# Attention, RWKV-7 and MoE block on one core: side steps without products ordered apart from PSUM places, x for the norm loaded piece by piece

## The chip, the core and the metric

One core of one Trainium2 chip runs the whole program. The metric is the device time of one execution in microseconds (us); lower is better. A change of 0.5% is 5.3 us here.

The core has engines that run beside each other, each with a queue of its own: PE (matrix products, with its weight loads listed as PEld), DVE, ACT and POOL (elementwise work, each with its own strengths), SP (issues DMAs). An engine takes its instructions strictly in the order of its queue; one that waits for data, for a place in SRAM or in PSUM (the accumulators of PE) holds up whatever stands behind it. ACT, POOL and SP issue DMAs too ("ACTq", "POOLq", "SPq" in the rows).

## The reference

One layer on `x` of 256 tokens by 2048 channels, all in float32:

```python
h = rms_norm(x, g_mix)
proj = h @ w_in                                   # all columns of both head groups
y_dsa = dsa_mixer(q, k, v, q_idx, k_idx, w_idx)   # indexer, top-k keys, rope, softmax
y_rwkv = rwkv7_mixer(r, d_w, k, v, d_a, d_g, ...) # state scan over the tokens, 16 heads x 64
x = x + concat([y_dsa, y_rwkv]) @ w_out
x = x + hier_moe(rms_norm(x, g_ffn))              # top-1 of 4 groups, top-2 of 4 experts in it
```

`rms_norm(x)` is x times `rstd`, one number per token: one over the root of the mean square over the 2048 channels. The kernel multiplies x by the weights first and by `rstd` behind the product, so the product need not wait for `rstd`.

## The kernel before

**Two stages.** Up to about 585 us the kernel does the projection, both mixers and the output projection; after that the MoE, expert pair by expert pair. The change touches the first stage alone.

**The stream.** The first stage is one long list of tasks, `stream`. A task of the first kind multiplies x (already scaled by the gain, in `hT0` to `hT3`) with one block of 128 columns, 12 products of 128x256 per task and four tasks per block; a task of the second kind takes 512 columns, 6 products of 128x512 per task and 16 tasks per 512 columns. Each product is made of three, since each operand is split into a high and a low part. `drive` walks over the tasks. It loads the raw weights with SP, 512 KB at a time (two tasks), into three places in turn (`RA` has two, `RB` one; line 210); it splits each half into a high part (ACT, the cast of line 222) and a low part (DVE, the subtraction of line 223), which stand in four halves of `W20` and `W21`, so that the split runs at most four tasks ahead of PE; and it lets PE multiply (`pp`, line 146).

**Side chains.** All else in that stage is done by Python generators ("chains") whose steps are laid between the tasks: `spread` (the norm's `rstd`), the low-rank parts, indexer and attention, and per RWKV block b an early part, a solve and a late part. The class `Order` holds a modelled time `t` that each product moves on. A step ends with `yield`: a number is a delay, so many microseconds of `t` until the next step, a name is an event to wait for. `run_ready` goes through the chains in the list's order and lets the first one run whose time has come; `ready` also asks for a place in PSUM: there are three for side products (`BANKS`), taken in turn, and one is counted free some time after the step that used it. The order on PE is exactly the order in which this plan writes the products; SP's loads and the steps on ACT, DVE and POOL follow the program too, but a scheduler may move them past each other.

**The norm.** `spread` (lines 288 to 312) loads x in four pieces of 512 KB by POOL (line 296) into `yr` and `qT`, which nothing else uses yet; ACT squares each piece into `vt` and sums along it (line 300); DVE and ACT make `rstd` (lines 302 to 304); DVE lays it on a diagonal (line 307); PE spreads it over the partitions (`rps`); ACT copies that to `rsB`. From then on each block's result waits for `rsB` and not for anything of `spread` again. On POOL, the loads of x share the queue with the rotary tables (lines 354 to 358).

**Solves.** `solve(b)` (lines 679 to 696) is a triangular solve on POOL, some 62 small operations; the result goes to DRAM (`dout`, line 695). `solved(b)` waits `SOLVE_US` of modelled time, and then has SP load it back into `XT` (line 702), four loads that stand in SP's queue between the weights'; `rwkv_late(b)` waits for that.

**Prefetch for the MoE.** After the last early part, `leave_rwkv` (lines 1159 to 1180) loads the first chunks of the experts' weights, 1 MB each; from then on `prefetch_step` (lines 1184 to 1193) is called at each weight load and adds a chunk when `PACE` says so. Each of these loads is gated: POOL copies one element of the current half of W (`pace["w"]`, set in `split`) into the new place before the load is issued, so that the load is not issued before ACT's cast into that half is done, and ACT's next cast into that half waits in turn for the copy (line 1145).

```python
c[0], c[1] = self.t + y, None              # a delay
c[0], c[1] = self.t, y                     # the name of an event
return None if r is None else max(r, self.free[self.place] or 0.0)
```

Of the kernel before, what the change touches and what calls it, by code (L numbers as in the profile page):

```python
# [9 lines left out]
F32 = mybir.dt.float32  # L10
F32R = mybir.dt.float32r
AF = mybir.ActivationFunctionType
# [5 lines left out]
P = 128  # L18
# [4 lines left out]
SB = 2  # L23
# [10 lines left out]
WARM = 14  # L34
BANKS, EMPTIED = 3, 2.0
PACE0 = 8.0
PACE, SOLVE_US, RSTD_US = 2.2, 39.0, 16.1
Y = [8.0, 5.6, 9.8, 1.6, 4.0, 2.6, 4.8, 5.8, 3.1, 6.0, 5.2, 3.0, 3.0, 3.1, 19.0, 5.7, 12.6, 4.4, 7.2, 4.8, 2.2, 6.6, 2.8, 6.2, 7.2, 2.2, 3.5, 0.0, 1.5, 1.1, 2.2, 16.1, 5.0, 2.2, 10.7, 10.4, 1.0, 5.0]

# [3 lines left out]
class Order:  # L45
# [18 lines left out]
    def event(self, name, delay=0.0):  # L64
        self.ev[name] = self.t + delay

    def add(self, gen):
        self.chains.append([0.0, None, gen])

    def ready(self, c):  # L70

        r = self.inputs(c)
        return None if r is None else max(r, self.free[self.place] or 0.0)

    def inputs(self, c):
        if c[1] is not None:
# [56 lines left out]
def block_kernel(ctx: ExitStack, tc: tile.TileContext, a: dict, dbg=None):  # L133
    nc = tc.nc
    PE, ACT, DVE, POOL, SP = nc.tensor, nc.scalar, nc.vector, nc.gpsimd, nc.sync
    SQ = POOL
    od = Order()
# [75 lines left out]
    pace = {}  # L213
# [19 lines left out]
    G = [gp.tile([P, 2048], F32, name=f"G{i}", tag=f"g{i}") for i in range(3)]  # L233
# [12 lines left out]
    state = rw.enter_context(tc.tile_pool(name="state", bufs=1, side="right"))  # L246
# [40 lines left out]

    def spread():

        yield 4.0  # L290
        part = const.tile([P, 2, 2], F32, name="part")
        xv = a["x"].rearrange("(j p) (c m) -> p j c m", p=P, c=2)
        xs = [t.rearrange("p b t -> p (b t)").rearrange("p (c m) -> p c m", c=2) for t in (yr, qT)]
        for j in range(2):
            for c in range(2):
                POOL.dma_start(out=xs[j][:, c, :], in_=xv[:, j, c, :])
                yield 1.0
        for j in range(2):
            for c in range(2):
                ACT.activation(out=vt[:, j, :], in_=xs[j][:, c, :], func=AF.Square, accum_out=part[:, j, c:c + 1])  # L300
                yield 1.0 * c
        DVE.tensor_tensor(out=rstd, in0=part[:, :, 0], in1=part[:, :, 1], op=ALU.add)
        ACT.activation(out=rstd, in_=rstd, func=AF.Ln, scale=1.0 / D, bias=eps6)
        ACT.activation(out=rstd, in_=rstd, func=AF.Exp, scale=-0.5)
        dg = temp("kd")
        for j in range(2):
            DVE.tensor_scalar(dg[:, j * P:(j + 1) * P], ident, rstd[:, j:j + 1], None, ALU.mult)
        yield 4.0
        ps = pbank("rps")
        mm(ps[:, 0:T], ones, dg)  # L310
        ACT.copy(out=rsB, in_=ps[:, 0:T])
        od.event("rsB", Y[22])

# [49 lines left out]
    yr = apool.tile([P, NB, T], F32, name="yr")  # L363
# [98 lines left out]
    def done0(ps):  # L462
# [7 lines left out]
        ACT.copy(out=SG[32:64, 2, :], in_=sgt[96:128, :])  # L470
        od.event("xb", Y[23])

    def done1(ps):
# [7 lines left out]
        for i in range(2):  # L481
            h = slice(64 * i, 64 * i + 64)
            ACT.copy(out=X1[h, i, :], in_=lo1[h, :])
            DVE.tensor_tensor(out=X1[64 - 64 * i:128 - 64 * i, i, :], in0=lo1[h, :], in1=X1[h, i, :].bitcast(F32), op=ALU.subtract)
        od.event("lo1", Y[24])

# [42 lines left out]
    def add_rwkv(b, which="krv"):  # L529
        for n, nm in enumerate("krv"):  # L530
            if nm not in which:
                continue
            def done(ps, n=n, nm=nm):
# [6 lines left out]
                shift(ps, 3 + 3 * b + n, t)  # L540
                od.event(f"{nm}{b}", Y[25])
            add_cm(3 + 3 * b + n, chain(done) if b == 0 else lambda ps, done=done: list(done(ps)))
# [12 lines left out]
    def rwkv_early(b):  # L555
# [4 lines left out]
        lh, ll = low_rank(b, 0, two_early)  # L560
        yield Y[0]
        pz = pbank("pz")
# [42 lines left out]
        r = s["r"]  # L605
# [13 lines left out]
        ACT.copy(out=rho, in_=KR[:, 1, :])  # L619

        AB = state.tile([P, 2, 4, 64], F32, name="AB", bufs=SB)
        MM = state.tile([P, 2, 4, 2, 64], F32, name="MM", bufs=SB + 1)
        pas = [pbank("pa") for _ in range(2)]
        od.emptied = 4.5
        for j in range(2):
# [12 lines left out]
        for ci in range(4):  # L638
            i = ci % 2
            ACT.dma_start(out=dr[b][0].rearrange("ci u s t -> ci s u t")[ci],  # L640
                           in_=AB[32 * ci:32 * ci + 32].rearrange("p h (j s) t -> p (h j) s t", s=2)[:, :, 0, 32 * i:32 * i + 32])
# [30 lines left out]
        for hj in range(4):  # L672
            h, j = hj // 2, hj % 2
# [7 lines left out]
    def solve(b):  # L681

        at = [tmp.tile([P, n, 32], F32, name=f"at{n}", bufs=1) for n in (8, 24)]
        xt = tmp.tile([P, 4, 32], F32, name="xt", bufs=1)
        tt = tmp.tile([P, 128], F32, name="tt", bufs=1)
        for t, r0, r1 in ((at[0], 0, 8), (at[1], 8, 32)):
            SQ.dma_start(out=t, in_=dr[b][0][:, :, r0:r1, :].rearrange("(o ci) u s t -> o (ci u) (s t)", o=1).broadcast_to([8, 16, 32 * (r1 - r0)]))
        POOL.tensor_copy(xt, xt0)
        for s_ in range(31):
            n, m = s_ // 8 + 1, 31 - s_  # L690
            tv = tt[:, 0:n * m].rearrange("p (u t) -> p u t", u=n)
            POOL.tensor_tensor(out=tv, in0=xt[:, 0:n, s_:s_ + 1].broadcast_to([P, n, m]),  # L692
                               in1=at[s_ >= 8][:, s_ % 8 if s_ < 8 else s_ - 8, s_ + 1:32].rearrange("p (o t) -> p o t", o=1).broadcast_to([P, n, m]), op=ALU.mult)
            POOL.tensor_tensor(out=xt[:, 0:n, s_ + 1:32], in0=xt[:, 0:n, s_ + 1:32], in1=tv, op=ALU.subtract)  # L694
        SQ.dma_start(out=dr[b][1].rearrange("ci w (i q) t -> q (ci w) i t", q=8), in_=xt.rearrange("p i t -> p (i t)"))
        od.add(solved(b))

    def solved(b):

        yield SOLVE_US  # L700
        for ci in range(4):
            tc.keep_in_program_order(SP.dma_start(out=XTs[b % SB][32 * ci:32 * ci + 32, :, 32 * ci:32 * ci + 32], in_=dr[b][1][ci].rearrange("u s t -> s u t")))
        od.event(f"solved{b}", Y[37])
# [107 lines left out]
    qT = apool.tile([P, 8, T], F32, name="qT")  # L811
    vt = apool.tile([P, 2, 1024], F32, name="vt")
# [179 lines left out]
    def put_heads():  # L992
        for h in range(4):
            yield f"att{h}"
            yield f"slot{YSLOTS.index(f'h{h}') // 4}"
            put_y(f"h{h}", qT[:, h, :])


    def chain(gen):
        return lambda ps: od.add(gen(ps))  # L1000
# [43 lines left out]
    od.add(kidx())  # L1044
    od.add(indexer())
    od.add(attention())
    od.add(put_heads())
    if dbg == "dsa":
        drive()
        od.finish()  # L1050
# [108 lines left out]
    def leave_rwkv():  # L1159

        yield f"early{NB - 1}"
        for i in range(2):
            load_chunk(i, True)
            yield PACE0

        x01 = mo_["x01"] = gp.tile([P, 2, 2, 512], F32, name="x01", tag="g2")
        POOL.tensor_copy(x01[0:1, 0, 0, 0:1], pace["w"][0:1, 0:1].bitcast(F32))
        for cc in range(2):
            POOL.dma_start(out=x01[:, cc], in_=a["x"].rearrange("(j p) m -> p j m", p=P)[:, :, cc * 512:(cc + 1) * 512])
        yield PACE0  # L1170
        yield f"late{NB - 1}"
        yield Y[19]
        rw.close()
        ewp[1] = ctx.enter_context(tc.tile_pool(name="ew", bufs=1, side="right", reuse_waits="tile"))
        for i in range(FIRST):
            load_chunk(2 + i)
        od.event("rw closed")
# [82 lines left out]

    c0, c1 = stream[-64:-48], stream[-48:-32]
    stream[-64:-32] = c0[:12] + c1[:8] + c0[12:] + c1[8:]
    od.add(leave_rwkv())
    drive(prefetch_step)
    od.finish()
    gF = mo_["gF"]
# [371 lines left out]
```

## Time and profile before

| what | value |
|---|---|
| median of 3 runs | 1054.12 us (1052.23 to 1056.83) |
| the profiled execution | 1053.52 us, its span 1051.7 us |
| PE busy | 1012.2 us, 96% of the span, 6476 products |
| DVE busy | 528.9 us (50%) |
| ACT busy | 387.7 us (37%) |
| POOL busy | 257.8 us (25%) |
| DMA | 298.75 MB, mean 284 GB/s |

The span runs from the first to the last instruction on the core; the execution's own time lies 1.8 us above it. PE is busy nearly all the time, so a few places where PE waits are all that a change of order can win or lose. A wait on an engine other than PE costs only where PE in the end waits for it.

### The profile page before, as it was taken

The numbers are of one execution on the slowest core, as the hardware profiler recorded it, in microseconds if no ns is written. First come the engines' busy times: TensorE is split into PE (matmuls) and PEld (weight loads), VectorE is DVE, ScalarE is ACT, GpSimd is POOL, SyncE is SP. The second block draws the span as 40 slices with busy tenths as digits, with TensorE's granted clock in tenths as the row PEclk, the third lists the DMA queues.
The fourth block names the chain that finished last, engine by engine and source line by source line (L and its number), as shares of the span: only waits on it lengthen the run. The fifth ranks groups of instructions, "written<-read, shape, count | busy, mean of one in ns | idle before, by whom it ended". The sixth has DMA issues, their size and how long they took to land.

```text
span 1051.7 us, 17181 instructions
## 1 busy us (share of the span) xinstructions
PE 1012.2 (96%) x6476; PEld 683.2 (65%) x6476; DVE 528.9 (50%) x1155; ACT 387.7 (37%) x836; POOL 257.8 (25%) x645
## 2 busy tenths in 40 slices
PE   5899999999999999999999899999999999999995
PEld 5898888889889877788877544444444444444432
DVE  5696787698978765756554313131312222221303
ACT  5666656566566754566454101010101010000001
POOL 3206676572664737002222110000000000000000
PEclk9999999999999999999999999999999999999999
DMA  8556744535454464648899798999999999999995
GB/s 286 211 180 174 203 150 136 167 114 147 134 155 139 137 189 133 235 123 289 285 324 378 314 365 352 422 419 420 420 421 419 421 420 420 419 421 420 420 405 176
DMA packets 69210, 298.75 MB, mean 284 GB/s; under 512 B 17184, under 2 KB 20048, under 8 KB 45056
## 3 DMA queue, kind: packets, MB, share of 16 engines
q1 hardware_dynamic: 54864, 248.59, 63.6%
q0 software_dynamic: 8928, 47.41, 12.7%
q10 hardware_dynamic: 5328, 1.58, 0.6%
q8 instruction: 53, 0.87, 0.3%
q14 instruction: 37, 0.30, 0.1%
HBM read 294.37 MB, written 3.15 MB: 283 GB/s over the span
## 4 chain that ended last, share of the span: by engine, by line
PE 78%; DVE 8%; DMA 5%; ACT 3%; issue 2%; POOL 2%; SPq 0%; ACTq 0%; DVEq 0%; POOLq 0%
PE pp L146 27%; PE pd L146 11%; PE gate L146 11%; PE up L146 10%; PE misc L146 6%; PE sc L146 3%; DVE W L223 3%; PE pz L146 2%; DMA RB<-wo 2%; PE py L146 2%; DMA RB<-wr 1%; POOL xt L694 1%; ACT W L222 1%; POOL tt L692 1%; DMA xT<-xT 1%
## 5 line engine op out<-in xcount | busy, mean ns | idle before, releaser
L146 PE MATMUL pp<-W,hT 128*128 128x512 f32 x768 | 190.1, 397 | 0.0
L146 PE MATMUL pp<-hT,W 128*128 128x256 f32 x1296 | 170.9, 289 | 11.8 <-DVE W L223 8.4
L223 DVE TENSOR_TENSOR W<-RA,W 128x512 fp32r<-128x512 f32 x200 | 138.3, 701 | 81.6 <-ACT W L222 80.9
L146 PEld LDWEIGHTS pp<-hT,W 128*128 128x128 f32 x1296 | 161.8, 194 | 16.2 <-DVE W L223 9.2
L222 ACT CAST W<-RA 128x512 fp32r<-128x512 f32 x200 | 121.8, 618 | 100.9 <-PE pp L146 52.2
L146 PEld LDWEIGHTS pp<-W,hT 128*128 128x128 f32 x768 | 139.8, 188 | 29.0 <-issue 0.7
L692 POOL TENSOR_TENSOR tt<-xt,at 128x24 f32<-128x24 f32 (+23 forms) x248 | 87.5, 353 | 52.5 <-DMA at<-din 33.7
L694 POOL TENSOR_TENSOR xt<-xt,tt 128x24 f32<-128x24 f32 (+23 forms) x248 | 94.4, 381 | 19.5
L146 PE MATMUL pp<-W,yT 128*128 128x512 f32 x384 | 91.3, 394 | 2.1 <-DVE W L223 2.1
L223 DVE TENSOR_TENSOR W<-RB,W 128x512 fp32r<-128x512 f32 x100 | 69.1, 696 | 48.3 <-ACT W L222 48.1
L146 PE MATMUL pd<-ew,R 128*64 128x512 f32 (+1 forms) x368 | 81.3, 580 | 2.0 <-DVE Y L1482 1.4
L222 ACT CAST W<-RB 128x512 fp32r<-128x512 f32 x100 | 61.2, 618 | 59.1 <-PE pp L146 28.3
L146 PEld LDWEIGHTS pp<-W,yT 128*128 128x128 f32 x384 | 71.0, 188 | 18.4 <-DVE W L223 3.6
L146 PE MATMUL up<-ew,R 128*64 128x512 f32 x352 | 79.3, 592 | 0.0
L146 PEld LDWEIGHTS misc<-sel,uu 128*128 128x128 f32 x512 | 60.1, 191 | 18.8 <-issue 13.8
L1491 ACT ACTIVATE Y<-pd,sv 128x512 fp32r<-128x512 f32 x31 | 21.3, 688 | 134.0 <-PE pd L146 134.0
L146 PE MATMUL misc<-sel,uu 128*128 128x128 f32 x512 | 64.9, 280 | 2.8 <-DVE R L1396 2.1
L1501 DVE TENSOR_TENSOR x<-x,sc 128x512 f32<-128x512 f32 (+1 forms) x58 | 36.2, 666 | 57.3 <-PE sc L146 57.3
L1396 DVE TENSOR_TENSOR R<-misc,gF 128x512 f32<-128x512 f32 x28 | 19.4, 692 | 87.1 <-PE misc L146 87.1
L146 PE MATMUL gate<-ew,R 128*64 128x512 f32 x272 | 61.7, 595 | 0.0
L1492 DVE SCALAR_TENSOR_TENSOR Y<-pd,sv,Y 128x512 fp32r<-128x512 f32 x31 | 23.3, 751 | 73.2 <-ACT Y L1491 73.2
L1420 ACT CAST selT<-misc 128x256 fp32r<-128x256 f32 x8 | 3.0, 372 | 153.7 <-PE misc L146 153.7
(389 smaller groups left out, 1216.4 us busy)
## 6 DMA issues: line engine op xcount, KB each, us to landing
ew<-we SPq DMA_DIRECT2D x66, 1024.0 KB, 19.9
ew<-wdn SPq DMA_DIRECT2D x38, 1024.0 KB, 19.3
ew<-we POOLq DMA_DIRECT2D x25, 1024.0 KB, 7.5
ewh<-we SPq DMA_DIRECT2D x24, 1024.0 KB, 18.2
RA<-wd SPq DMA_DIRECT2D x43, 512.0 KB, 3.8
RA<-wr SPq DMA_DIRECT2D x35, 512.0 KB, 3.9
RB<-wd SPq DMA_DIRECT2D x21, 512.0 KB, 3.7
RA<-wo SPq DMA_DIRECT2D x21, 512.0 KB, 4.6
```

The lines of the kernel that those rows point to most:

```text
L146: PE.matmul(out, lhsT=lhsT, rhs=rhs, start=start, stop=stop, skip_group_check=skip)
L222: ACT.copy(out=hi, in_=raw)
L223: DVE.tensor_tensor(out=lo, in0=raw, in1=hi.bitcast(F32), op=ALU.subtract)
L692: POOL.tensor_tensor(out=tv, in0=xt[:, 0:n, s_:s_ + 1].broadcast_to([P, n, m]), in1=at[s_ >= 8][:, s_ % 8 if s_ < 8 else s_ - 8, s_ + 1:32 ...
L694: POOL.tensor_tensor(out=xt[:, 0:n, s_ + 1:32], in0=xt[:, 0:n, s_ + 1:32], in1=tv, op=ALU.subtract)
L1396: DVE.tensor_tensor(out=t[:, a:b], in0=ps.rearrange("p (a t) -> p a t", t=P)[:, a:b], in1=gF[:, 4 * kq + a:4 * kq + b].rearrange("p (a o) ...
L1420: ACT.copy(out=selT, in_=ps[:, 0:T])
L1491: ACT.activation(out=yh, in_=pd, func=AF.Copy, scale=sv[:, 1:2])
L1492: DVE.scalar_tensor_tensor(out=yl, in0=pd, scalar=sv[:, 1:2], in1=yh.bitcast(F32), op0=ALU.mult, op1=ALU.subtract)
L1501: DVE.tensor_tensor(out=x1[j][:, ns], in0=(uu[:, j, ns] if first else x1[j][:, ns]), in1=ps, op=ALU.add)
```

## The change

- `add` takes a flag `dry`. A dry chain is one without products: `solved`, `put_heads` and `leave_rwkv`. It no longer asks for a place in PSUM before it runs, and stands at the front of the list of chains, not at its end.
- `spread` takes its x in four pieces into other places: three tiles `xs` that share their ring with `MM` (a tile of the early part), and the right half of `G1`. Each load is gated by POOL's copy of one element of the current half of W, as the prefetches are. The steps that issue the loads are 2 us of modelled time apart, and the squares are written in place of the pieces.
- Numbers: `PACE` from 2.2 to 1.8, `SOLVE_US` from 39 to 41, and five of the delays `Y`: `Y[3]` (1.6 to 2.4), `Y[8]` (3.1 to 3.4), `Y[12]` (3.0 to 3.6), `Y[16]` (12.6 to 13.2), `Y[37]` (5.0 to 4.5).

```diff
-PACE, SOLVE_US, RSTD_US = 2.2, 39.0, 16.1
-Y = [8.0, 5.6, 9.8, 1.6, 4.0, 2.6, 4.8, 5.8, 3.1, 6.0, 5.2, 3.0, 3.0, 3.1, 19.0, 5.7, 12.6, 4.4, 7.2, 4.8, 2.2, 6.6, 2.8, 6.2, 7.2, 2.2, 3.5, 0.0, 1.5, 1.1, 2.2, 16.1, 5.0, 2.2, 10.7, 10.4, 1.0, 5.0]
+PACE, SOLVE_US, RSTD_US = 1.8, 41.0, 16.1
+Y = [8.0, 5.6, 9.8, 2.4, 4.0, 2.6, 4.8, 5.8, 3.4, 6.0, 5.2, 3.0, 3.6, 3.1, 19.0, 5.7, 13.2, 4.4, 7.2, 4.8, 2.2, 6.6, 2.8, 6.2, 7.2, 2.2, 3.5, 0.0, 1.5, 1.1, 2.2, 16.1, 5.0, 2.2, 10.7, 10.4, 1.0, 4.5]
...
-    def add(self, gen):
-        self.chains.append([0.0, None, gen])
+    def add(self, gen, dry=False):
+
+        c = [0.0, None, gen, dry]
+        self.chains.insert(0, c) if dry else self.chains.append(c)
 
     def ready(self, c):
 
         r = self.inputs(c)
-        return None if r is None else max(r, self.free[self.place] or 0.0)
+        return r if r is None or c[3] else max(r, self.free[self.place] or 0.0)
...
     def spread():
 
-        yield 4.0
         part = const.tile([P, 2, 2], F32, name="part")
         xv = a["x"].rearrange("(j p) (c m) -> p j c m", p=P, c=2)
-        xs = [t.rearrange("p b t -> p (b t)").rearrange("p (c m) -> p c m", c=2) for t in (yr, qT)]
-        for j in range(2):
-            for c in range(2):
-                POOL.dma_start(out=xs[j][:, c, :], in_=xv[:, j, c, :])
-                yield 1.0
-        for j in range(2):
-            for c in range(2):
-                ACT.activation(out=vt[:, j, :], in_=xs[j][:, c, :], func=AF.Square, accum_out=part[:, j, c:c + 1])
-                yield 1.0 * c
+        xs = [state.tile([P, 1024], F32, name="xs", tag="MM", bufs=SB + 1) for _ in range(3)] + [G[1][:, 1024:2048]]
+        yield 3.0
+        for n in range(4):
+            POOL.tensor_copy(xs[n][0:1, 0:1], pace["w"][0:1, 0:1].bitcast(F32))
+            POOL.dma_start(out=xs[n], in_=xv[:, n // 2, n % 2, :])
+            yield 2.0
+        yield 1.0
+        for n in range(4):
+            ACT.activation(out=xs[n], in_=xs[n], func=AF.Square, accum_out=part[:, n // 2, n % 2:n % 2 + 1])
+            yield 1.0 * (n % 2)
...
-        MM = state.tile([P, 2, 4, 2, 64], F32, name="MM", bufs=SB + 1)
+        MM = state.tile([P, 2, 4, 2, 64], F32, name="MM", tag="MM", bufs=SB + 1)
...
-        od.add(solved(b))
+        od.add(solved(b), dry=True)
...
-    od.add(put_heads())
+    od.add(put_heads(), dry=True)
...
-    od.add(leave_rwkv())
+    od.add(leave_rwkv(), dry=True)
```

**POOL, at the start of the program** (the rows after its first memsets and loads; `cs` and `gq` are tables for the rotation, `cg` and `sg` what is made of them, `xt` the start of a solve). Lines 297 and 298 of the changed kernel are the gate's copy and the load of x. Before:

```order
L575 MEMSET G1_89 128x4
L296 DMA yr_190<-x 128x1024 x2
L296 DMA qT_214<-x 128x1024 x2
L346 DMA cs64_184<-cs64 128x128
L354 ISA
L354 TENSOR_TENSOR cg_182<-cs128_641,gq_642 128x64
```

Of the changed kernel, from the second of its last table operations on:

```order
L358 TENSOR_SCALAR sg__183<-sg__183 128x64
L690 COPY xt_986<-con_174 128x128
L298 DMA xs_222<-x 128x1024
L297 COPY xs_223<-W21_84 1x1
L358 TENSOR_SCALAR sg__183<-sg__183 128x64
L359 TENSOR_SCALAR sn64_185<-cs64_184 128x2x32
L360 COPY sn64_185<-cs64_184 128x2x32
L297 COPY xs_224<-W20_83 1x1
L297 COPY G1_89<-W20_83 1x1
L358 TENSOR_SCALAR sg__183<-sg__183 128x64
L298 DMA xs_223<-x 128x1024
L298 DMA xs_224<-x 128x1024
```

The four loads of x stood ahead of all table operations; now the first stands behind 19 of them and the last at their end, the copy of the first gate being the eighth of the operations.

**PE, around the product that spreads `rstd`** (`rps`; each row x12 is one task). Before:

```order
L146 MATMUL pp_348<-hT1_69,W20_83 128x256 x12
L146 MATMUL pp_348<-hT2_70,W21_84 128x256 x12
L146 MATMUL pp_348<-hT3_71,W21_84 128x256 x12
L146 MATMUL rps_410<-G0_88 128x256
L146 MATMUL pp_415<-hT0_68,W20_83 128x256 x12
```

Of the changed kernel:

```order
L148 MATMUL pp_351<-hT3_71,W21_84 128x256 x12
L148 MATMUL pp_419<-hT0_68,W20_83 128x256 x12
L148 MATMUL pp_419<-hT1_69,W20_83 128x256 x12
L148 MATMUL pp_419<-hT2_70,W21_84 128x256 x6
L148 MATMUL rps_455<-G0_88 128x256
L148 MATMUL pp_419<-hT2_70,W21_84 128x256 x6
```

Two and a half tasks have moved from behind `rps` to ahead of it: 14½ stand ahead of it instead of 12.

**SP, around the loads of the fourth solve's result** (`dout3`; `wr` and `wd` are weights of the stream, `lora` the low-rank weights). Before:

```order
L210 DMA RB_82<-wr 128x1024
L210 DMA RA_81<-wr 128x1024 x2
L210 DMA RB_82<-wr 128x1024
L210 DMA RA_81<-wd 128x1024
L702 DMA XT1_187<-dout3_204 32x4x32 x4
L210 DMA RA_81<-wd 128x1024
```

Of the changed kernel:

```order
L508 DMA G1_89<-lora 128x256
L212 DMA RA_81<-wr 128x1024 x2
L704 DMA XT1_187<-dout3_204 32x4x32 x4
L212 DMA RB_82<-wr 128x1024
L212 DMA RA_81<-wr 128x1024 x2
L212 DMA RB_82<-wr 128x1024
L212 DMA RA_81<-wd 128x1024 x2
```

The four loads of `dout3` go ahead of five weight loads that they stood behind.

## Rows read from the trace of the kernel before

**Rows 1.** The page's head: the span, and each engine's busy time.

```profile
span 1051.7 us, 17181 instructions
PE 1012.2 (96%) x6476; PEld 683.2 (65%) x6476; DVE 528.9 (50%) x1155; ACT 387.7 (37%) x836; POOL 257.8 (25%) x645
```

**Rows 2.** Waits by what ended them: us in total, times, longest us.

```profile
PE pp L146 <- DVE W L223: 10.5, 6, 7.0
...
PE rps L146 <- DVE G L307: 2.8, 1, 2.8
PE tps L156 <- DVE re L742: 2.2, 1, 2.2
...
PE pz L146 <- DVE R L728: 1.1, 1, 1.1
```

**Rows 3.** Timeline, the way to `rps`: start, us, engine, operation, [idle before <- what ended it].

```profile
19.78 1.06 POOL L296 DMA_DIRECT2D yr<-x  x2 [16.01 <-DMA G<-lora]
20.14 8.89 PE L146 MATMUL pp<-hT,W 128*128 128x256 f32 x72 [0.21 <-DVE W L223]
...
22.52 0.53 POOL L354 TENSOR_TENSOR cg<-cs,gq 128x64 f32<-128x64 f32 x1
...
24.48 0.76 POOL L355 TENSOR_TENSOR sg__183<-cs,gq 128x64 f32<-128x64 f32 x1
...
27.99 0.31 POOL L355 TENSOR_TENSOR sg__183<-cs,gq 128x64 f32<-128x64 f32 x1
...
29.10 1.40 DVE L223 TENSOR_TENSOR W<-RB,W 128x512 fp32r<-128x512 f32 x2 [4.03 <-ACT W L222]
...
29.93 1.45 POOL L356 TENSOR_SCALAR sg__183<-sg__183 128x64 f32<-128x64 f32 x3
...
31.71 1.06 ACT L300 ACTIVATE vt<-qT 128x1024 f32<-128x1024 f32 x1
...
35.82 0.67 PE L146 MATMUL rps<-G 128*128 128x256 f32 x2 [2.82 <-DVE G L307]
```

**Rows 4.** DMA issues: KB each, median us from issue to landing.

```profile
RB<-wr SPq DMA_DIRECT2D x18, 512.0 KB, 4.1
...
yr<-x POOLq DMA_DIRECT2D x2, 512.0 KB, 5.2
qT<-x POOLq DMA_DIRECT2D x2, 512.0 KB, 9.1
```

**Rows 5.** Timeline, the first gated chunk, behind the last solve.

```profile
415.23 0.19 POOL L1145 COPY ew<-W 1x1 f32<-1x1 f32 x1
415.45 0.62 ACT L222 CAST W<-RB 128x512 fp32r<-128x512 f32 x1 [6.41 <-POOL ew L1145]
```

**Rows 6.** Timeline, the end of the output projection on PE.

```profile
577.93 1.65 PE L146 MATMUL pp<-W,yT 128*128 128x512 f32 x6 [1.57 <-DVE W L223]
```

**Rows 7.** The chain of waits at that place: start, us, what.

```profile
567.12 9.30 DMA RB<-wo
```

**Rows 8.** Timeline around the end of the fourth solve.

```profile
232.72 0.33 SPq L210 DMA_DIRECT2D RB<-wr  x1
...
237.54 0.29 POOL L688 COPY xt<-con 128x128 f32<-128x128 f32 x1 [3.45 <-DMA dout<-xt]
...
241.59 0.62 ACT L222 CAST W<-RB 128x512 fp32r<-128x512 f32 x1 [0.81 <-PE pp L146]
```

**Rows 9.** Windows: us; busy us (count) of PE, PEld, DVE, ACT, POOL; PEclk, DMA share, GB/s.

```profile
12.40:16.40 4.00, 4.00 (x19) 3.87 (x19) 3.68 (x9) 3.63 (x9) 0.00 (x0) 1.00 1.02 393
20.50:24.50 4.00, 4.00 (x36) 4.00 (x35) 3.65 (x10) 2.40 (x5) 3.90 (x8) 1.00 0.81 271
...
775.00:800.00 25.00, 24.65 (x138) 11.63 (x135) 4.06 (x11) 1.65 (x3) 0.00 (x0) 1.00 1.01 420
1048.00:1051.70 3.70, 0.00 (x0) 0.00 (x0) 0.00 (x0) 0.00 (x0) 0.00 (x0) 0.50 0.06 13
```

**Rows 10.** Timeline, the last products of the program.

```profile
1043.58 0.74 PE L146 MATMUL sc<-Y,selT 128*128 128x256 f32 x4 [1.00 <-DVE Y L1482]
```

## The prediction, made before the changed kernel ran

> **What bounds the kernel now.** I read the page's head first: PE is busy for 1012.2 us of 1051.7 [rows 1]. A change of order can therefore only win or lose at the few places where PE waits, and the list of waits names them. The largest is `pp` behind DVE's split, 10.5 us in six waits of which 7.0 is one [rows 2], at the program's start, where the first weights have not landed; the change does not reach it. The others that it touches are 2.8 us at `rps`, 2.2 at `tps`, 1.1 at `pz` and 1.57 at the end of the output projection [rows 2, 6]. The MoE stage is dense: 24.65 of 25 us with DMA at 420 GB/s [rows 9]; none of its instructions is moved, so it shifts with the first stage. All sums are against the profiled execution, 1053.52 us, which lies 0.6 below the median of the runs, 1054.12.
>
> **Term 1, the way to `rstd`: +3.7 us.** Before, the loads of x were the first thing that POOL did at 19.78, two of them in 1.06 us, so 0.53 each, and the first table operation followed at 22.52 [rows 3]. Twelve tasks stood ahead of `rps`, eight of them behind 20.14. Six took 8.89 us, so 1.48 each [rows 3]; eight need 11.8, and `rps` could have begun at 32.0. It began at 35.82: the stretch lost 3.8 us.
> Now the tables go first. Only the load of `cs64` is ahead of them, so they begin about 2.1 us earlier (four loads of 0.53), at 20.4. From 22.52 to 29.93 POOL did what now stands ahead of the first load of x [rows 3], 7.4 us; that ends at 27.8. But a table operation takes 0.76 us at 24.48, in a stretch where DVE is busy 3.65 of 4.00 us [rows 9], and 0.31 at 27.99, while DVE stands idle for the 4.03 us before 29.10 [rows 3]; starting earlier, some three more fall beside splits, 0.45 each, and the gate copies are 0.2 each [rows 5]. So the first piece is issued at about 30. Behind it come three operations like those at 29.93 (0.48 each), two small ones, three gate copies and three loads: the last piece is issued at about 34. The landing is unknown in its new place: 4.1 to 9.1 us are the bounds [rows 4]; I take 6, near `yr`'s 5.2, since these four share with weight loads and come closer together. The last piece is there at 40, and its square takes 1.06 us and 0.2 for the sum [rows 3]: 41.3. From the last square to `rps` it took 2.9 us before, with two casts between, 0.6 each [rows 5]; none stands between now, so 1.8, and `rps` begins at 43.1. Its 14½ tasks would have let it begin at 20.14 + 10.5 x 1.48 = 35.7, so 7.4 us are lost where 3.8 were: **+3.7**, rounded up. In it lie PE's waits for four casts that now wait for gate copies; ACT holds splits back there, which costs no more than `rps` does anyway. Bounds: with every operation at 0.31 and a landing of 4.1 the last piece is there by 36 and the term is -0.5; with 9.1 it is 3.1 more, and with what else may slip +7.
> [...] By the rows DVE itself runs dry while ACT's casts wait, as before 29.10, and I keep three; the slower case is the third rival.
>
> **Term 2, the gate behind the last solve: -1.4 us.** The first chunk's gate copy stands behind the solve on POOL, at 415.23; ACT's next cast waits 6.41 us for it [rows 5], and PE behind that for 2.2 at `tps` [rows 2]. In the new order the products that start this solve stand 4.1 us of stream work earlier, and the cast that waits is two splits earlier, worth 2.7; the solve wins by the difference, 1.4. Bounds 0 and -2.2.
>
> **Term 3, the delays `Y` and the side chains: 0.** `pz` waits 1.1 us for DVE [rows 2], at a step whose delay `Y[8]` is raised by 0.3; a similar raise stands in `Y[3]`, `Y[12]`, `Y[16]`. I take 1.0 off. The late chains of blocks 5 to 7 now stand 4 to 5.5 us of stream work earlier, and steps that come earlier can wait anew, as `pz` did: 1.0 on, between 0 and 4. `put_heads` and `solved` without a place change when SP is asked, not what PE does: that costs nothing as long as the weight loads' lead covers it (second rival).
>
> **Term 4, the end of the output projection: -1.5 us.** PE waits 1.57 us [rows 6] for a weight load that took 9.30 us [rows 7] where 4.1 is usual [rows 4], amid a burst of 1 MB chunks. At `PACE` 1.8 one chunk more is loaded ahead of the burst, so one fewer lies in it. Bounds +1.6 (the wait doubles: the same bytes come in a shorter stretch) and -1.6.
>
> **Sum.** 3.7 - 1.4 + 0 - 1.5 = +0.8: 1054.3 for an execution like the profiled one, 1054.9 on the scale of the median. The forecast is **1055.0 us**, no measurable change: 0.5%, 5.3 us, is about what a measurement of this kernel can tell from none. Its own range is 1052 to 1058.5, from the middle parts of these bounds.
>
> **Rivals.**
> *The clock falls at `rps`.* Of the 7.4 us lost some 2 lie at the casts behind the gates and about 5.4 in one wait at `rps`. [...] Against it: the wait of 2.8 us before `rps` did not bring it down, the 72 products of 20.14 and those behind `rps` run alike. At 12.40, early in the program, 19 products took the 4.0 us in which 36 ran later [rows 9]: half speed, though that row's clock reads 1.00; that row alone cost 2.0. The same here gives **1057.0**. [...]
> *Slower: SP stands at `dout3`.* Its four loads now go ahead of five weight loads. SP would come to them before the load at 232.72, and stand until the solve's result has landed at 237.54, when POOL's next operation, which waits for it too, runs; with about 2 us for the four, the weight load of 232.72 is issued at 239.6, 6.9 late [rows 8]. Its cover: its cast came at 241.59, 8.9 behind the issue, of which 4.1 is landing [rows 4, 8], so 4.8; the splits are three tasks ahead of PE, 4.4, less 1.3 for the split itself (0.62 and 0.70 [rows 3, 5]). That makes 7.9, **1.0 us more than needed**. For the cover: the first pieces of that chain are where they were in the stream. Against it: if this solve comes 4 us later against the stream, as the chains of the first blocks do, PE waits 3 us here and 2 at the next one (`dout4`, three loads earlier): 1055 + 5 = **1060**. It decides where the solve ends over 1 us later than before against the load at 232.72.
> *POOL is held longer.* If all eleven operations between the first gate and the first load take 0.76 and not 0.31 [rows 3], that is 5.0 us where I took 1.4: x comes 3.6 later, **1058.6**. For it: ACT has four splits' work in hand when the tables begin; against it: the gates stop ACT, and so DVE, soon after.
> *Faster: all waits go.* POOL's table operations run at 0.31, x lands in 4 to 5 us, and terms 2 to 4 reach their lower bounds: -0.5 - 2.2 - 1.1 - 1.6 = -5.4, **1048.7**; half way, 1051.5.
> *The change does not do what it says*: the order itself shows all four parts moved, so I give this nothing.
>
> **How the numbers follow.** Forecast 0.42, clock 0.22, SP 0.14, POOL held 0.08, all waits gone 0.14. Of the last, half lies below 1048.9 (1054.12 less 5.3): faster 0.07, and 0.01 of the forecast's, 0.08. Above 1059.4 lie 0.09 of SP, 0.03 of POOL held, 0.04 of the clock's (with term 1 in its upper half) and 0.02 of the forecast: slower 0.18. The rest, 0.74, is the same. The range 1050 to 1061 takes in the forecast, the clock, most of SP and of POOL held, and some half of the last; left out are about 0.06 below and 0.10 above.
>
> **What would show it.** The trace after would have: x's first load on POOL at about 30 and the last at 34; `rps` at 43 with PE idle for about 5 us before it; ACT's wait for the first chunk's gate at 5 us; no wait of over 1 us behind `wo` loads; SP idle behind `dout3`, with no wait of PE for `RB` following. Products behind `rps` at twice their spacing speak for the clock. `rps` before 40, or PE waits of over 3 us at any place from 100 to 560 us, would prove the sum wrong.

## The result, and the profile of the changed kernel

The changed kernel took **1082.47 us** (median of four, 1080.76 to 1086.26) where the kernel before took 1053.44 beside it: a ratio of 1.0278, 95% interval 1.0252 to 1.0304. It is 29 us slower; the forecast was 1055.0 and the range ended at 1061. (In one run below, the new numbers alone, one of the four executions fell into a slow state, at 1455.97 us; it stands in the median there, but not in the ratio.) The head of the page answers to [rows 1]:

```profile
span 1079.9 us, 17153 instructions
...
PE 1024.3 (95%) x6476; PEld 692.1 (64%) x6476; DVE 530.3 (49%) x1155; ACT 386.4 (36%) x836; POOL 257.7 (24%) x649
```

Two subtractions say a good deal. The span is 28.2 us longer. PE's busy time, for the same 6476 products, is 12.1 us longer (1024.3 against 1012.2); what is left of the span, PE's idle time, is 16.1 us longer (55.6 against 39.5). So PE did not only wait more, it also ran the same products slower. The list of waits names the idle part, beside [rows 2]:

```profile
PE pp L148 <- DVE W L225: 20.9, 9, 7.3
PE rps L148 <- DVE G L309: 8.1, 1, 8.1
PE pz L148 <- DMA XT<-dout: 4.4, 1, 4.4
...
PE ips L148 <- ACT kt__3264 L662: 1.7, 1, 1.7
```

`pp` went from 10.5 to 20.9, `rps` from 2.8 to 8.1; the waits for `XT` and of `ips` are new, 4.4 and 1.7. The windows show where, and the slower running too. Of the changed kernel, around `rps`, around the first solve's late part, and behind the fourth solve (columns as in [rows 9]; the column that reads 0.79, 0.87, 0.80 is the granted clock):

```profile
28.00:52.00 24.00, 14.44 (x101) 14.09 (x102) 10.52 (x22) 13.96 (x29) 4.44 (x10) 0.79 0.50 177
126.00:152.00 26.00, 21.58 (x121) 17.49 (x121) 11.79 (x23) 10.50 (x22) 16.14 (x51) 0.87 0.51 143
256.00:290.00 34.00, 25.50 (x205) 22.79 (x205) 16.27 (x39) 12.60 (x26) 12.23 (x35) 0.80 0.45 130
```

The same times in the kernel before (not quite the same work, since it was further on by then):

```profile
28.00:52.00 24.00, 20.34 (x165) 19.87 (x164) 16.97 (x34) 16.32 (x34) 4.79 (x12) 1.00 0.57 203
126.00:152.00 26.00, 26.00 (x193) 21.91 (x193) 20.34 (x39) 16.59 (x35) 21.61 (x57) 1.00 0.53 162
256.00:290.00 34.00, 34.00 (x280) 29.10 (x281) 31.77 (x81) 20.24 (x46) 23.05 (x64) 1.00 0.50 139
```

In each of the three, PE stands for a while and the granted clock reads below 1.00. Before, it read 1.00 in all three. Shorter windows behind the waits of the changed kernel read 0.50, with PE busy all through them; the fourth lies behind a shorter wait at the third place, the 1.7 us of `ips`:

```profile
44.50:48.00 3.50, 3.50 (x15) 3.32 (x16) 1.33 (x4) 1.50 (x4) 0.00 (x0) 0.50 0.01 2
139.10:143.00 3.90, 3.90 (x13) 3.50 (x14) 0.00 (x0) 0.58 (x1) 2.96 (x13) 0.50 0.16 60
267.70:273.00 5.30, 5.30 (x24) 5.00 (x24) 4.57 (x15) 0.05 (x1) 0.00 (x0) 0.50 0.36 111
277.10:280.40 3.30, 3.30 (x16) 3.30 (x16) 2.00 (x4) 1.93 (x4) 2.35 (x7) 0.50 0.72 227
```

These hold 16.0 us of busy PE with the clock at 0.50. If half of that would do where it reads 1.00, as for the eight `pz` products of place 2 below (1.05 us against 2.05), about 8 of the 12.1 us lie here (an estimate).

**Place 1, `rps`.** The timeline of the changed kernel: when the first and the last piece of x were asked for, the last square, and the product.

```profile
27.23 0.60 POOL L298 DMA_DIRECT2D xs<-x  x1
...
30.97 0.53 POOL L298 DMA_DIRECT2D G<-x  x1
...
41.72 1.06 ACT L302 ACTIVATE G<-G 128x1024 f32<-128x1024 f32 x1 [1.39 <-DMA G<-x]
...
44.29 1.20 PE L148 MATMUL rps<-G 128*128 128x256 f32 x2 [8.09 <-DVE G L309]
```

The view of DMA issues gives the landings, beside 5.2 and 9.1 in [rows 4]:

```profile
xs<-x POOLq DMA_DIRECT2D x3, 512.0 KB, 6.4
...
G<-x POOLq DMA_DIRECT2D x1, 512.0 KB, 10.7
```

The 9.1 is the median of two pieces; the view of the tile `qT` in the kernel before, up to 60 us, has both, and the longer is the last of the four:

```profile
DMA to landing us min/median/max: 8.0/9.1/10.3
```

**Place 2, the first solve.** PE reaches the late part (`pz`) 49 us behind the solve's products (`pa`) and waits 4.42 us for the result:

```profile
85.31 1.10 PE L148 MATMUL pa<-G 64*64 64x128 f32 x32
...
139.10 2.05 PE L148 MATMUL pz<-R,XT 128*128 128x128 f32 x8 [4.42 <-DMA XT<-dout]
```

In the kernel before the same two stood 55.5 us apart, and nothing waited; the same eight products took 1.05 us there and 2.05 here:

```profile
74.14 1.10 PE L146 MATMUL pa<-G 64*64 64x128 f32 x32
...
129.64 1.05 PE L146 MATMUL pz<-R,XT 128*128 128x128 f32 x8
```

**Place 3, the fourth solve.** SP's timeline of the changed kernel, beside [rows 8]:

```profile
236.09 4.55 SPq L212 DMA_DIRECT2D RA<-wr  x2
258.89 2.12 SPq L704 DMA_DIRECT2D XT<-dout  x4
261.12 0.38 SPq L212 DMA_DIRECT2D RB<-wr  x1
```

SP is through with `RA` at 240.6 and issues nothing for 18.2 us; it stands at `dout3`, as SP's list of waits says (us in total, times, longest):

```profile
SPq L704 <- DMA dout<-xt: 27.5, 3, 18.2
```

The weight load behind it goes out at 261.12; ACT's cast waits for that load, and PE for the split:

```profile
266.22 1.14 ACT L224 CAST W<-RB 128x512 fp32r<-128x512 f32 x2 [11.10 <-DMA RB<-wr]
```

```profile
257.84 3.03 PE L148 MATMUL pp<-hT,W 128*128 128x256 f32 x24
267.62 2.71 PE L148 MATMUL pp<-hT,W 128*128 128x256 f32 x11 [6.75 <-DVE W L225]
```

The solve itself had begun its work late: POOL waited longer for its data (`at`) to land, in the kernel before and then in the changed one:

```profile
203.88 0.24 POOL L692 TENSOR_TENSOR tt<-xt,at 128x31 f32<-128x31 f32 x1 [2.52 <-DMA at<-din]
```

```profile
225.24 0.78 POOL L694 TENSOR_TENSOR tt<-xt,at 128x31 f32<-128x31 f32 x1 [6.57 <-DMA at<-din]
```

### The profile page after: what moved, and what is told of

The parts are those of the page before. It is cut to its first block, busy times and chain, and to the rows that moved or that the text cites. A ratio compares the mean times of both kernels' runs of the same rounds, so it can differ in the third digit from the quotient of the medians.

```text
span 1079.9 us, 17153 instructions
## 1 busy us (share of the span) xinstructions
PE 1024.3 (95%) x6476; PEld 692.1 (64%) x6476; DVE 530.3 (49%) x1155; ACT 386.4 (36%) x836; POOL 257.7 (24%) x649
## 4 chain that ended last, share of the span: by engine, by line
PE 68%; DMA 13%; DVE 6%; POOL 6%; issue 2%; ACT 2%; ACTq 1%; SPq 1%; POOLq 0%; DVEq 0%
PE pp L148 25%; PE gate L148 9%; PE up L148 9%; PE pd L148 8%; PE misc L148 5%; PE sc L148 3%; POOL tt L694 2%; POOL xt L696 2%; DMA ew<-wdn 2%; DMA ew<-we 2%; DMA eww<-we 2%; DVE W L225 2%; PE pz L148 2%; DMA RB<-wr 1%; DMA at<-din 1%
## 5 line engine op out<-in xcount | busy, mean ns | idle before, releaser
L148 PE MATMUL pp<-hT,W 128*128 128x256 f32 x1296 | 175.5, 294 | 18.0 <-DVE W L225 17.3
L148 PEld LDWEIGHTS pp<-hT,W 128*128 128x128 f32 x1296 | 166.1, 198 | 22.0 <-DVE W L225 18.4
L694 POOL TENSOR_TENSOR tt<-xt,at 128x24 f32<-128x24 f32 (+23 forms) x248 | 90.7, 366 | 53.6 <-DMA at<-din 34.8
L696 POOL TENSOR_TENSOR xt<-xt,tt 128x24 f32<-128x24 f32 (+23 forms) x248 | 88.9, 359 | 19.5
L1493 ACT ACTIVATE Y<-pd,sv 128x512 fp32r<-128x512 f32 x31 | 21.3, 687 | 134.2 <-PE pd L148 134.2
```

Source lines behind the costliest of these rows:

```text
L148: PE.matmul(out, lhsT=lhsT, rhs=rhs, start=start, stop=stop, skip_group_check=skip)
L1493: ACT.activation(out=yh, in_=pd, func=AF.Copy, scale=sv[:, 1:2])
```

## The experiments

Two theories stood at first. *Two causes*: the late x costs on its own, and the dry chains on their own, since a solve's result is asked for too early. *One cause*: the late `rstd` sets PE back, and the later waits follow from that. Every time is a median beside the kernel before on the same chip; the ratios are formed from the executions themselves, so they can differ by some tenths of a per cent from the quotient of the two medians.

**Each part alone, and the change without the dry flags.** First the kernel before with the new loading of x:

```diff
+        xs = [state.tile([P, 1024], F32, name="xs", tag="MM", bufs=SB + 1) for _ in range(3)] + [G[1][:, 1024:2048]]
...
+            POOL.tensor_copy(xs[n][0:1, 0:1], pace["w"][0:1, 0:1].bitcast(F32))
+            POOL.dma_start(out=xs[n], in_=xv[:, n // 2, n % 2, :])
```

> The kernel before with only the new loading of x (gated pieces into other places, the shared ring). Theory 'two causes' (the late x costs on its own and the missing PSUM condition on its own): rps waits about 8 us, half clock for some 4 us behind it, so 9 to 10 us over the kernel before, about 1063; no wait of PE at XT<-dout, and SP's wait for dout under 3 us. Rival 'one cause' (the late rstd pushes every later solve against the stream, and the later waits follow from it): here too PE waits some 4 us for XT at the first solve and 7 us for a weight load behind the fourth, about 1078.

Measured: 1061.97 beside 1050.65, ratio 1.010 (1.0073 to 1.0128). `rps` waits 7.9 us, SP does not wait for `dout`, `XT` is waited for 3.5 us in two waits of at most 1.9. Around `rps` the clock reads 0.86:

```profile
28.00:52.00 24.00, 14.39 (x101) 14.04 (x102) 10.48 (x22) 13.92 (x29) 4.70 (x12) 0.86 0.52 179
```

So the new loading of x costs 11 us by itself, and the long later waits do not follow from it.

Next, `add` and `ready` of the change with the three flags, and nothing else:

```diff
-        od.add(solved(b))
+        od.add(solved(b), dry=True)
...
-    od.add(put_heads())
+    od.add(put_heads(), dry=True)
...
-    od.add(leave_rwkv())
+    od.add(leave_rwkv(), dry=True)
```

> The kernel before with only the dry chains (no place in PSUM asked for, front of the list), old numbers, old loading of x. Its order puts the first solve's products 237 stream products behind the solve's start where before had 264 and the changed kernel 243, and SP's loads of the third and fourth result 7 weight loads earlier than before. Theory 'two causes': rps as before (2.8 us), but PE waits 5 to 7 us for XT at the first solve and at least 7 us for a weight load behind the fourth solve, each with half clock behind it: 15 to 25 us over before, 1069 to 1079. Rival 'one cause': about 1054, since x comes as before.

Measured: 1071.61, ratio 1.0178 (1.0145 to 1.0210). x comes as before (`rps` waits 3.2), and the time still rises by 21 us. `XT` is waited for 6.2 us in two waits, 3.4 at the first solve; SP waits for `dout` at every solve:

```profile
SPq L704 <- DMA dout<-xt: 46.4, 8, 11.3
```

The expected 7 us wait for a weight load did not come; PE waited 5.5 at `pa` and 4.1 at `tps` instead. The sum was right, the places in part.

Third, the new numbers alone:

```diff
-PACE, SOLVE_US, RSTD_US = 2.2, 39.0, 16.1
+PACE, SOLVE_US, RSTD_US = 1.8, 41.0, 16.1
...
```

> The kernel before with only the new numbers (PACE 1.8, SOLVE_US 41, five delays Y). Theory 'two causes': nothing is put ahead of its solve; within 3 us of before, 1051 to 1056. Rival 'the numbers did it' (steps that come earlier by the new delays are the ones that wait): over 1060.

Measured: 1063.42, ratio 1.0110 (1.0075 to 1.0146). The theory missed: the numbers alone cost 11 to 13 us. In its profile there are a wait of 2.3 us for `XT` and 14.2 us at `pp` where before had 10.5; what ties them to the new numbers is not shown.

Last, the changed kernel without the flags:

```diff
-        od.add(solved(b), dry=True)
+        od.add(solved(b))
...
-    od.add(put_heads(), dry=True)
+    od.add(put_heads())
...
-    od.add(leave_rwkv(), dry=True)
+    od.add(leave_rwkv())
```

> The changed kernel with the dry flags taken away (solved, put_heads and leave_rwkv ask for a PSUM place again), all else as changed. First solve's products stand 309 stream products behind its start. Theory 'two causes': what is left is the late x with its clock, 1060 to 1065; no PE wait at XT, SP's wait for dout under 3 us. Rival 'one cause': still over 1072.

Measured: 1076.64, ratio 1.0245 (1.0202 to 1.0289). Again a miss. SP no longer waits for `dout`, but `XT` is waited for 6.0 us in three waits and `pn` for 1.9. Here x and the numbers make 26 us, about the 11 and 13 that they made alone; with the flags on top it is 29, though the flags alone made 21. So 'one cause' falls with the first run, and 'two causes' as it stood with the third: the numbers are one too, and the parts do not add, since each lays the whole plan anew. PE waits for a solve's result in all four runs (3.5, 6.2, 2.9 and 6.0 us in total); SP waits for one only where the flags are set. The next runs moved one step at a time.

**The solves, one at a time.** First all of them:

```diff
-PACE, SOLVE_US, RSTD_US = 1.8, 41.0, 16.1
+PACE, SOLVE_US, RSTD_US = 1.8, 48.0, 16.1
```

> The changed kernel with SOLVE_US 48 for 41, so that a solve's result is asked for 7 us of modelled time later; SP's loads of the results stand 2, 2, 3 and 4 weight loads later. Theory 'dry chains are asked for too early': no wait of PE at XT over 1 us, SP's wait for dout under 5 us in all, no 7 us wait behind the fourth solve; what the late x and the numbers cost stays, 1064 to 1070. Rival (any new laying of the side steps costs, wherever the solves stand): 1074 to 1080 with waits at other side steps.

Measured: 1066.54 beside 1052.18, ratio 1.0104 (1.0045 to 1.0163); 15 us of the 29 are gone by the medians, 18 by the ratio. `XT` is waited for 1.2 us, SP does not wait for `dout` any more, `rps` still waits 7.9.

Then the fourth alone, which leaves PE's order as it is in the changed kernel:

```diff
-        yield SOLVE_US
+        yield SOLVE_US + 7.0 * (b == 3)
```

> The changed kernel with the fourth solve alone asked for 7 us of modelled time later: the four loads of dout3 stand behind four weight loads more on SP, and nothing else moves on any engine, PE's order is that of the changed kernel. Theory (SP standing at dout3 holds the weight load back, and PE waits and falls to the lower clock): SP's longest wait for dout falls from 18 us to under 3, the 6.9 us wait of pp behind it and the half clock of 260 to 280 us go, the stream gains 12 to 15 us at that place, 1067 to 1071. Rival (PE waits there for the solve's own data or a late early part of the next block): the gain is under 5 us, 1077 or more.

Measured: 1073.52 beside 1053.68, ratio 1.0183 (1.0151 to 1.0215): 9 us of the 29 are gone, a little less than expected. (A few neighbours on ACT and DVE did swap places.) The place itself is healed:

```profile
256.00:290.00 34.00, 33.61 (x327) 29.77 (x327) 28.50 (x74) 21.31 (x50) 19.52 (x55) 1.00 0.46 124
```

SP's longest wait for `dout`, now at another solve, is 7.7 us instead of 18.2 and covered. Place 2 is untouched in it, `XT` still waited for 4.6 us. With the order on PE the same, this shows that SP's standing at `dout3` was what held PE.

Then the first and the fourth:

```diff
-        yield SOLVE_US
+        yield SOLVE_US + 7.0 * (b in (0, 3))
```

> The changed kernel with the first and the fourth solve alone asked for 7 us of modelled time later; the first solve's late part stands at stream product 729 instead of 702. If the wait of 4.4 us at XT behind the first solve, with its half clock, is the other half of what SOLVE_US 48 for all gained: 1064 to 1068, no wait at XT over 1.5 us and the granted clock at 1.00 from 126 to 152 us. If that place is bound otherwise (the wait only moves): 1071 to 1074 as with the fourth solve alone.

Measured: 1063.13 beside 1052.53, ratio 1.0093 (1.0062 to 1.0124). That is 18 us of the 29, so the first and the fourth solve account for all that moving every solve gained. But this run, unlike the one before, changes the order on PE from the first late part on, so that the wait at place 2 alone made the other 9 us is not shown as cleanly. The clock is back at place 2:

```profile
126.00:152.00 26.00, 24.64 (x137) 20.29 (x137) 16.77 (x32) 14.75 (x31) 16.08 (x46) 1.00 0.65 176
```

**The late x.** The kernel before with the new `spread`, less the gates:

```diff
-            POOL.tensor_copy(xs[n][0:1, 0:1], pace["w"][0:1, 0:1].bitcast(F32))
             POOL.dma_start(out=xs[n], in_=xv[:, n // 2, n % 2, :])
```

> The kernel before with the new places for x but without the gates: the four loads stand on POOL ahead of the tables and wait for nothing, all else as in the run with only the new loading of x. Theory (gates and tables make x late): rps waits under 3 us and the 8 us and the half clock go, while 2 MB more in the first 10 us make the first weights up to 5 us later: 1050 to 1056. Rival (x is late by its landing, 9 to 11 us among the weight loads, whoever asks for it): still 1058 to 1063.

Measured: 1056.51 beside 1052.18, ratio 1.0024 (0.9999 to 1.0049), 4.3 us over the kernel before, where the same kernel with gates lay 11.3 over it. x is asked for at 1.88 us, `rps` does not wait at all, and the price is paid at the start: the first products wait 7.0 us for `hT`, where before it was 3.4.

```profile
PE pp L146 <- ACT hT L285: 7.0, 3, 3.8
```

Then both remedies in the changed kernel, SOLVE_US 48 and no gates:

> The changed kernel with SOLVE_US 48 and without the gates on the loads of x: both causes taken away, dry chains, PACE and the delays Y as changed. If the two causes add, the run without gates has shown some 5.5 us and SOLVE_US 48 some 16: 1082.5 less 21, 1059 to 1063; rps waits under 2 us, SP's wait for dout under 5 us. If one hides the other, over 1064.

Measured: 1058.23 beside 1053.68, ratio 1.0045 (1.0027 to 1.0063). Here the causes add: 24 of the 29 us are gone. The solves gave back 15 to 18 of them by themselves, and the gates some 7. The last 4 to 5 us remain; the numbers and the first products, which wait 6.1 us for `hT` here, are candidates, and their shares are not shown.

**The numbers.** PACE alone (2.2 to 1.8 in the kernel before):

> The kernel before with PACE 1.8 alone; the order on PE is that of before, only the prefetched chunks come earlier. Theory (faster chunks take bandwidth from the last weight loads): waits of PE behind the splits at the end of the output projection grow by 3 to 6 us, 1054 to 1058 beside a kernel before of 1051. Rival (the term of the prediction): one chunk fewer in the last burst, 1 to 2 us less than before.

Measured: 1056.64 beside 1052.18, ratio 1.0027 (1.0006 to 1.0049). The expected price came, the expected place did not: at the end of the output projection two waits make 1.92 and 1.36 us, little more than before.

```profile
571.73 3.02 PE L146 MATMUL pp<-W,yT 128*128 128x512 f32 x12 [1.92 <-DVE W L223]
...
582.00 1.67 PE L146 MATMUL pp<-W,yT 128*128 128x512 f32 x6 [1.36 <-DVE W L223]
```

In its profiled execution the first solve's products begin at 77.12, 3 us later than in the kernel before, where PACE plays no part yet. Where its 4 us come from stays open.

The delays and SOLVE_US alone, with PACE 2.2:

```diff
-PACE, SOLVE_US, RSTD_US = 2.2, 39.0, 16.1
+PACE, SOLVE_US, RSTD_US = 2.2, 41.0, 16.1
...
```

> The kernel before with the new delays Y and SOLVE_US 41, and PACE left at 2.2. The run with all numbers lay 11 to 12 us over before and the one with PACE alone 4 to 5. If PACE and the delays add: 1059 to 1062, waits at wo weight loads as before. If the delays alone did it: 1063 to 1066.

Measured: 1061.27 beside 1052.53, ratio 1.0086 (1.0057 to 1.0114). With PACE's 4 the delays make what all numbers made. In its windows the first solve's place is hurt again, by a wait of 1.8 us for `XT`. That wait and its clock do not make 9 us; where the rest comes from stays open.

```profile
126.00:152.00 26.00, 24.20 (x141) 20.07 (x140) 16.59 (x33) 14.56 (x29) 20.46 (x58) 0.93 0.53 158
```

**The clock's share.** The changed kernel with PE kept busy through the wait at `rps`:

```diff
         ps = pbank("rps")
+        for _ in range(32):
+            PE.matmul(ps[:, T:T + P], lhsT=ones, rhs=ones, start=True, stop=True, skip_group_check=False)
```

> The changed kernel with 32 products of 128x128 on constants put into the wait ahead of rps, into a part of its place in PSUM that nothing reads; what is computed stays the same. Theory 'each wait is paid twice' (PE waits, then runs at the lower clock): rps begins as late as in the changed kernel, about 44, but the granted clock stays at 1.00 from 40 to 50 us and the stream is 3 to 4 us ahead of the changed kernel's by 52 us; 1077 to 1080 if the later places lose what they lost. Rival (the lower clock costs nothing, since splits and x are late anyhow): the stream stands where the changed kernel's stood at 52 us, 1082.

Measured: 1085.63 beside 1052.18, ratio 1.0289 (1.0238 to 1.0341), no gain on the whole, where 1077 to 1080 had been expected. At the place itself the effect is plain. The first 8 us from `rps` on, in the changed kernel and then with the filling:

```profile
44.30:52.30 8.00, 8.00 (x50) 7.82 (x51) 5.57 (x12) 5.34 (x12) 0.94 (x1) 0.74 0.04 12
```

```profile
47.00:55.00 8.00, 8.00 (x68) 7.95 (x67) 6.41 (x13) 6.08 (x13) 0.85 (x1) 1.00 0.19 68
```

68 products instead of 50: with 8.00/68 us each, the lower clock behind `rps` costs 18 x 0.118 = 2.1 us. That much and more went back at the start, where `rps` came 2.7 us later in this execution (46.99 against 44.29), and it is less than the spread of the runs (1081.39 to 1086.79).

The same in the kernel before, with 14 products for 32:

> The kernel before with 14 products on constants (3.2 us) put into its own wait ahead of rps; what is computed stays the same and nothing else moves on PE. Theory (some executions fall to the lower clock behind the 2.8 to 4 us wait at rps): the granted clock stays 1.00 from 30 to 50 us in every profile, and the time falls by 1 to 2 us against before. Rival (the filling ends later than the wait by about half a us, and the clock mostly holds anyway): no change within 1 us.

Measured: 1051.36 beside 1053.81, ratio 0.9985 (0.9967 to 1.0003): 1 to 2 us less, as expected, and the interval just reaches no change. The clock reads 1.00 around `rps` (28 to 52 us). It is the fastest kernel of this study, by an amount that can't be told from nothing.

**The gate behind the last solve**, the prediction's term 2, taken away in the kernel before for the first chunk:

```diff
-            load_chunk(i, True)
+            load_chunk(i, i > 0)
             yield PACE0
```

> The kernel before with the first prefetched chunk's gate taken away (its load goes out ahead of the last solve instead of behind it), PE's order unchanged. Theory: ACT's cast no longer waits 6.4 us for POOL, the 2.2 us of PE at tps go, and 1 MB more is loaded early: 1 to 3 us less than before. Rival: the second chunk's gate takes the first one's place behind the same solve, same as before within 1 us.

Measured: 1057.46 beside 1053.68, ratio 1.0032 (1.0013 to 1.0051): slower, where 1 to 3 us less had been expected. The wait at `tps` is gone, but the chunk of 1 MB now goes out among the loads of the seventh solve's result, and PE waits there:

```profile
384.23 0.58 POOL L1149 DMA_DIRECT2D ew<-we  x1 [0.18 <-ACT kt__5016 L660]
386.69 2.25 SPq L702 DMA_DIRECT2D XT<-dout  x4
...
397.10 1.82 PE L146 MATMUL pz<-R,XT 128*128 128x128 f32 x8 [3.36 <-DMA XT<-dout]
```

## Why the prediction was wrong

Three steps failed. The one that weighs most is term 3, which put the earlier loads of the solves' results at nothing: moving the solves back was worth 15 to 18 of the 29 us. Next comes term 1, where the new loading of x cost 11 us by itself for the 3.7 forecast. Third, the sum priced each wait at its length and left out the slower products behind it. PE waits of over 3 us between 100 and 560 us, the prediction's own sign of a wrong sum, came twice, 4.42 and 6.75.

- **Term 1: right in its mechanism, one part mis-sized.** The queue on POOL was reckoned well: the first piece was issued at 27.23 and the last at 30.97 in an execution whose stream began 2.1 us earlier (18.04 against 20.14), that is 9.2 and 12.9 us behind it, where "about 30" and "about 34" are 9.9 and 13.9. The landing failed: "I take 6", with 9.1 as the upper bound, and the last piece took 10.7. The kernel before had shown as much: its four pieces, too, were issued right behind each other, each took longer to land than the one before it (4.7, 5.8, 8.0 and 10.3 us), and the 9.1 of [rows 4] is the median of the last two. The last of the four took 10.3 there (place 1 above). `rstd` waits for the last piece, so that was the figure to take, and not `yr`'s 5.2. `rps` waited 8.1 us, not about 5.4. By the prediction's own reckoning the way to `rps` lost 10.7 us (44.29 less 18.04 is 26.25; 10.5 tasks need 15.5) where 3.8 were lost before: +6.9 against +3.7, just its upper bound. The part alone cost 11 us; of the 4 between, about 2.1 are the lower clock behind `rps` (0.74 in its first 8 us), and the rest stays open.
- **The clock was a rival and is a term.** It was offered with 0.22 as another way in which things go, and priced at 2.0 for one place. It fell, at `rps` for about that price (2.1 us), which is luck: the 2.0 came from a stretch whose clock read 1.00 [rows 9]. It fell at the two other places too (0.87 and 0.80 in their windows). No wait of the kernel before had shown it: there the clock reads 1.00 in every 8 us up to 1040. PE's busy time, in which the slower products show, is 12.1 of the 28.2 us; about 8 of it lies in the windows at 0.50 above. The step that failed is the sum, in which a wait was priced at its own length.
- **Term 3 failed outright: "`put_heads` and `solved` without a place change when SP is asked, not what PE does".** `solved` also makes the event that lets the late part go. With the flag it is no longer held up by PSUM (the flags alone gave a wait of 3.4 us for `XT`), and `pz` comes 49.4 us behind the solve's products and not 55.5; the solve and its loads took 53.8. The working counted how far each chain had moved in the stream, never the distance from a solve's start to the demand for its result. (The flags alone cost 21 us. Taking them out of the changed kernel gave back only 3, since the other parts then lay the plan in yet another way.)
- **The rival at SP named the place, and missed the size.** SP stood at `dout3`, a weight load came late and PE waited. Its cover, 7.9 us, was about right: in the run with the fourth solve alone moved, the same weight load went out at 248.29 with the next block's `pa` at 259.72; with `pa` at 256.46 in the changed kernel that is 245.0, so 261.12 is 16.1 us late, and PE waited 6.75, 9.4 less. But the rival let the solve end as before against the stream ("1.0 us more than needed"), or 4 us later. It landed at 258.89, 21.3 later than before, while that `pa` came 13.6 later (256.46 against 242.88), so 8 us later against the stream. About half of that arose at the solve's start, where POOL waited 6.57 us and not 2.52 for the solve's data (`at`, place 3 above). The rival had 0.14, and its price of 5 us was 9.
- **Term 2 was right**: ACT's wait for the gate fell from 6.41 to 5.47 us, about the 5 that was forecast, and the wait of 2.2 at `tps` is gone (none there is over 0.3). **Term 4 was not**: the last waits at `wo` loads did not shrink (1.92 and 1.19 us now, with one of 0.17 between; 0.50 and 1.57 before).
- **The numbers were costed at nothing** but for term 4; alone they cost 11 to 13 us, the delays (with `SOLVE_US`) some 9 of it. By what mechanism stays open, but for one wait at the first solve.
- The cases were laid side by side as if one of them would come true. Late x, the clock and SP came together, and their prices added: the range ended at 1061, since each was added to the forecast alone.

The rival with POOL held longer did not come: of the eleven operations between the first gate and the first load two took 0.85 and 0.87 us and nine 0.31 to 0.36, and POOL issued the first piece 9.2 us behind the start of the stream, where 9.9 had been reckoned with three of them slow.

## What to carry to other kernels

In an order that was laid by hand, a condition that seems only to hold a step back (here the place in PSUM) may be the margin that lets its data arrive: before removing it, compare for each consumer the time from the start of the work to the demand with the time the work needs, queue by queue. A load that waits for a result must not stand ahead of loads that PE needs sooner. And where PE is the bound, price a wait at its length and at the slower products behind it (here 8.1 us at `rps` and about 2.1 behind it), and add the cases that can come together.

## What was not expected of the hardware

In the changed kernel PE ran slower behind the wait at each of the three places (8.1, 4.4 and 6.75 us, the clock at 0.50 behind each), so that the wait cost more than its length. But that was not always so: behind 2.8 us at `rps` the clock read 1.00 from 30 to 40 us in the kernel before, and 0.83 in the same stretch of two other kernels that waited 2.8 there too (the numbers alone, and the delays alone). In the changed kernel it read 0.50 even behind the 1.7 us at `ips`. Over the whole program PE's busy time grew by 12.1 us of 1079.9. And of four 512 KB pieces of x that POOL asked for within 4 us, the last took 10.7 us to land (10.3 in the kernel before), twice the 5.2 of the first pair before: what waits for all four waits for the last.
